# One trunk of two layers on one core: modulation sums of 1024 columns, two of them beside layer 0's modulation, paired scores, level factors from chunk tables, and eight weight pieces kept at the seam of the layers

## The chip, the core and the metric

The kernel runs on one core of a Trainium2 chip. TensorE multiplies (its weight loads are shown apart, as PEld), VectorE (DVE), ScalarE (ACT) and GpSimd (POOL) compute, SyncE (SP) issues nearly all DMAs from one queue. The metric is the device time of one execution in microseconds (us); a few runs agree within 0.3%.

## What is computed

A latent stream `x` of 256 tokens and a context of 256 tokens, 2048 features each, pass two layers. Each layer normalises, modulates, mixes, normalises again and adds to the stream:

```python
mod_l = silu_c @ w_mod[l] + b_mod[l]                 # shift, scale, gate: 3 x 2048
h_lat = rms_norm(x, g_pre[l]) * (1.0 + sc_l) + sh_l
y_lat = even_mixer(...) if l == 0 else odd_mixer(...)
x = x + gt_l * rms_norm(y_lat, g_post[l])
```

Layer 0's mixer has two branches from one projection of 9 x 1024 columns. One is differential attention with 8 heads: two softmaxes over 512 keys per head, each on 64 features, the second subtracted with a weight. The other is a gated linear recurrence (HGRN2) with 8 heads, run forwards and backwards; per head `exp(cumsum(log f))` weighs the keys and queries:

```python
att = jnp.einsum('bthk,btshk,bshk->bhts', qc, decay, kc)   # decay = exp(b_t - b_s), s <= t
s_new = jnp.exp(b_last)[..., None] * s + ...               # state over chunks of 32 tokens
```

The branches are gated and projected back to 2048 features. Layer 1 pools neighbouring tokens over 2, 4, 8 and 16 positions, with a projection before and after. All data are float32.

## The kernel before, in words

*Weight pieces.* A projection is a `Group` (L251): 512 output columns, accumulated in banks of PSUM over 8 pieces of 256 rows. `load_w` (L209) brings a piece of 512 KB by SP into one of four `w` buffers; `split` (L215) copies it to a rounded `hi` on ScalarE and subtracts on VectorE to get `lo`; `mul` (L265) makes three matmuls (L279) for each product: hi x hi, hi x lo, lo x hi. A piece has 12 matmuls of 512 columns for two token tiles, 24 for four.

*Order.* A scheduler orders each engine's instructions by priority and by the time at which it thinks them ready; `tc.high_priority(offset=...)` raises or lowers it (FILLB = -400 is low, CHAIN = 500 high). On the chip each engine keeps that fixed order. Beside the pieces of a group, `beside` (L406) steps two queues of generators: `bg`, the heads of a branch that is ready, and `fill`, modulation sums that are needed later. The numbers BD0, FD0, FH and so on (L48 to L50) are steps per piece.

*Modulation.* Layer 0's scale and shift come from `gemv` on TensorE (L305, matmuls at L318), whose 2 x 16 MB of weights are loaded in spans of 1, 1, 2, 4, 4 and 4 tiles of 128 features (`SPANS`, loop at L487). Between the loads of a span stand pieces of the three groups that start layer 0 (`starters`). The other rows, layer 1's scale and shift and both gates, come from `gemv_row` (L326): 8 loads of [256 rows x 512 columns] into two `wf` buffers, and for each row tile one instruction of VectorE that multiplies by the condition and adds to `ga` (L335, L337). A `feature_sink` (L347) then sums over partitions with small matmuls (L353), a `gate_sink` (L364) with one wide one (L374). There are 16 such rows of 512 columns; seven are queued after `hg_batch(0)` and stepped beside `da_batch(0)` and `hg_batch(1)`, five after that, four in layer 1.

*Recurrent heads* (`hg_heads`, L627, stepped beside `da_batch`). `b` is a cumulative sum that restarts every 32 tokens. The cross-half factor (level 128) and level 64 are scans of their own (`scan`, L572 to L576), `qi`, the factor of the state, two more. Levels 32 to 2 subtract on VectorE left and right halves apart (L602 to L606), exponentiate on ScalarE (L607), multiply by q (L624). Each level's 128x128 products (L648, L658) are merged into `att` on VectorE with a mask (`copy_predicated`, L663). The tag `tb` has 8 buffers.

*Attention heads* (`da_heads`, L725). For each head and token tile the scores of the two 64-feature halves (L735, three matmuls each into an `auxb` bank), maximum (L736), exponential (L740), difference (L747), transposes (L751) and the product with the values (L757), both in `auxb` too. `auxb`, `aux` have two banks each, `acc` four.

*The seam.* `close_layer` (L864) ends a layer: for the last group all pieces are first multiplied for token tile 0 and kept, then for tile 1, while tile 0 is scaled, added to the stream, squared and normalised (`normed`, L937, matmuls L944). Layer 1's first group (L967) keeps LAG = 3 pieces in the same way for tile 0 before tile 1 is there:

```python
            for k2 in range(LAG):
                kept.append((k2, g.weights(k2, where=in_y if k2 > 2 else None)))
                g.mul(*kept[-1], js=[0])
```

Of the kernel before, what the change touches and what calls it, by code (L numbers as in the profile page):

```python
# [46 lines left out]
LAG = 3  # L47
FH, FG, FO, FD0, FD1, FZ, FU = 2, .5, .5, .7, .7, .5, .5  # L48
# [6 lines left out]
def hybrid_kernel(  # L55
# [24 lines left out]
    def tinyb(n, dtype=F32):  # L80
        return alloc("tinyb", [P, n], dtype, 12)
# [111 lines left out]
    tmp = tiny(32)  # L193
# [54 lines left out]
    def in_y():  # L248
        return alloc("y", [P, 2, 512], F32R, 4), alloc("y", [P, 2, 512], F32R, 4)
# [76 lines left out]
    def gemv_row(l, col, sink):  # L326

        acc = alloc("ga", [P, 512], F32, 1)
        for k2 in range(8):
            w = load_w(w_mod[l], k2, col, "wf", 2)  # L330
            with tc.high_priority(offset=FILLB):
                for i in range(2):
                    sc = csil[:, 2 * k2 + i, 0:1]
                    if k2 + i == 0:
                        nc.vector.tensor_scalar(out=acc, in0=w[:, i, :], scalar1=sc, scalar2=None, op0=ALU.mult)  # L335
                    else:
                        nc.vector.scalar_tensor_tensor(out=acc, in0=w[:, i, :], scalar=sc, in1=acc, op0=ALU.mult,  # L337
                                                       op1=ALU.add)
            if k2 < 7:
                yield  # L340
# [23 lines left out]
    def gate_sink(l, f):  # L364
        def sink(ev):
            if f % 2 == 0:
                gtg[l, f // 2] = alloc("qT", [P, 1024], F32, 3)
            dst = gtg[l, f // 2][:, (f % 2) * 512:(f % 2) * 512 + 512]
            bb, gb = t2([P, 512]), t2([P, 512])
            cc = slice(f * 512, f * 512 + 512)  # L370
            nc.sync.dma_start(out=bb, in_=b_mod[l:l + 1, 4096 + f * 512:4608 + f * 512].to_broadcast([P, 512]))
            nc.sync.dma_start(out=gb, in_=g_post[l:l + 1, cc].to_broadcast([P, 512]))
            pt = aux([P, 512])
            nc.tensor.matmul(pt, ones[:, 0:P], ev, start=True, stop=True)  # L374
            nc.vector.tensor_tensor(out=dst, in0=pt, in1=bb, op=ALU.add)
            nc.vector.tensor_tensor(out=dst, in0=dst, in1=gb, op=ALU.mult)
        return sink
# [119 lines left out]
    work(len(pending))  # L497
# [3 lines left out]
    lvm = cst.tile([P, 8, P], U8, name="lvm")  # L501
    for i in range(0, 8, 4):
        t = t2([P, 4, P])
        nc.sync.dma_start(out=t, in_=lvlmask[:, i:i + 4, :])
        nc.vector.tensor_copy(out=lvm[:, i:i + 4, :], in_=t)
# [36 lines left out]
    def hg_logs(zc, d, gks, Ss, v_ctx):  # L542

        for h in range(4):
# [550 lines left out]
```

## Time and profile before

| | us |
|---|---|
| median of 3 runs | 1280.19 |
| lowest and highest | 1279.68, 1283.44 |
| profiled execution, its time | 1280.65 |
| profiled execution, its span | 1278.8 |
| TensorE busy | 1216.6 (95%) |
| VectorE busy | 937.1 (73%) |
| ScalarE busy | 588.1 (46%) |
| mean granted TensorE clock | 0.993 |

The span runs from the first to the last instruction; the execution's own time adds what lies around it. Busy shares are means over stages: the span has layer 0's modulation to about 228 us, layer 0's mixer to about 936 us, the seam to about 980 us and layer 1 after it. A matmul's busy time begins before the one ahead has ended, so the busy time of a row of matmuls is shorter than the sum of theirs; the granted clock is a share of full speed (1.00 is 2.4 GHz, 0.50 is 1.2).

### The profile page before, as it was taken

What the parts mean: (1) busy time and instruction counts of PE and PEld (TensorE: products, weight loads), DVE (VectorE), ACT (ScalarE), POOL (GpSimd) and SP (SyncE); (2) the same over time, 40 slices, a digit from 0 to 9 for tenths busy, and PEclk for the clock granted to TensorE, in tenths of its full rate; (3) what the DMA queues carried; (4) which work ended last, traced back from release to release, by engine and by line L of the source; (5) the groups of instructions that cost most, each with busy time, mean ns of one, the idle gap of its engine ahead of it and who ended that gap; (6) DMA issues with size and microseconds to landing.
All of it is one profiled execution on the core that took longest, in us unless ns stands there. A gap on an engine that the chain in (4) does not pass through costs nothing.

```text
span 1278.8 us, 16568 instructions
## 1 busy us (share of the span) xinstructions
PE 1216.6 (95%) x5938; PEld 958.7 (75%) x5938; DVE 937.1 (73%) x1711; ACT 588.1 (46%) x999; POOL 5.6 (0%) x59
## 2 busy tenths in 40 slices
PE   3999999999999999999999999999998999999997
PEld 2666677777788777777777777788876888888885
DVE  3554556999988656688899797888866668786654
ACT  4231324764544633234544456664456535444452
POOL 0000000000000000000000000000000000000000
PEclk9999999999999999999999999999998999999999
DMA  9988753753335447767445266767854788776553
GB/s 290 319 303 296 266 172 98 258 170 112 119 99 172 163 141 230 234 201 243 132 132 169 79 221 204 267 213 260 309 206 158 226 302 296 263 242 191 177 201 116
DMA packets 144246, 263.72 MB, mean 206 GB/s; under 512 B 8306, under 2 KB 21412, under 8 KB 144164
## 3 DMA queue, kind: packets, MB, share of 16 engines
q1 hardware_dynamic: 144164, 262.66, 61.9%
q8 instruction: 47, 0.77, 0.2%
q14 instruction: 35, 0.29, 0.1%
HBM read 260.53 MB, written 2.10 MB: 205 GB/s over the span
## 4 chain that ended last, share of the span: by engine, by line
PE 67%; DVE 16%; DMA 9%; ACT 4%; issue 3%; SPq 1%; DVEq 0%; ACTq 0%
PE acc L279 46%; PE auxb L279 8%; DMA wf<-in_w_mod_dram 5%; DVE lo L218 3%; DVE ga L337 3%; PE aux L318 3%; DVE tb L576 3%; PE auxb L658 2%; PE auxb L735 2%; ACT hi L217 2%; DMA h<-in_w_mod_dram 1%; PE auxb L757 1%; PE aux L353 1%; DMA w<-in_ev_w_out_dram 1%; DMA w<-in_ev_w_in_dram 1%
## 5 line engine op out<-in xcount | busy, mean ns | idle before, releaser
L279 PE MATMUL acc<-hi,h 128*128 128x512 f32 x1968 | 632.9, 396 | 1.0 <-ACT hi L217 1.0
L217 ACT ACTIVATE hi<-w 128x1024 fp32r<-128x1024 f32 x270 | 286.0, 1060 | 393.5 <-PE acc L279 254.8
L279 PEld LDWEIGHTS acc<-hi,h 128*128 128x128 f32 x1968 | 368.4, 188 | 84.5 <-issue 10.3
L218 DVE TENSOR_TENSOR lo<-w,hi 128x1024 fp32r<-128x1024 f32 x270 | 328.9, 1221 | 138.8 <-ACT hi L217 127.2
L279 PE MATMUL acc<-lo,h 128*128 128x512 f32 x984 | 389.1, 395 | 2.9 <-DVE lo L218 2.9
L279 PEld LDWEIGHTS acc<-lo,h 128*128 128x128 f32 x984 | 185.3, 188 | 46.2 <-issue 6.1
L337 DVE SCALAR_TENSOR_TENSOR ga<-wf,csil,ga 128x512 f32<-128x512 f32 x240 | 179.6, 748 | 46.1 <-DMA wf<-in_w_mod_dram 42.7
L279 PE MATMUL acc<-h,hi 128*128 128x512 f32 x512 | 165.9, 400 | 0.0
L279 PEld LDWEIGHTS acc<-h,hi 128*128 128x128 f32 x512 | 96.8, 191 | 19.2 <-issue 0.5
L279 PE MATMUL acc<-h,lo 128*128 128x512 f32 x256 | 102.4, 400 | 0.0
L279 PE MATMUL auxb<-h,hi 128*128 128x512 f32 x256 | 82.9, 405 | 1.1 <-DVE tb L300 1.1
L279 PEld LDWEIGHTS auxb<-h,hi 128*128 128x128 f32 x256 | 45.8, 188 | 25.2 <-issue 8.2
L300 DVE TENSOR_TENSOR tb<-auxb,tb 128x512 f32<-128x512 f32 x56 | 38.0, 688 | 30.1 <-PE auxb L279 30.0
L279 PEld LDWEIGHTS acc<-h,lo 128*128 128x128 f32 x256 | 49.0, 191 | 9.2
L279 PE MATMUL auxb<-h,lo 128*128 128x512 f32 x128 | 49.8, 394 | 0.0
L318 PE MATMUL aux<-h,tb 128*32 128x128 f32 (+2 forms) x320 | 30.1, 476 | 9.3 <-DMA h<-in_w_mod_dram 5.7
L658 PEld LDWEIGHTS auxb<-tb 128*128 128x128 f32 x224 | 29.8, 190 | 10.0 <-DVE tb L624 4.5
L658 PE MATMUL auxb<-tb 128*128 128x128 f32 x224 | 33.7, 282 | 1.2 <-DVE tb L624 0.8
L736 DVE TENSOR_REDUCE tinyb<-auxb 128x1 f32<-128x512 f32 x32 | 22.0, 687 | 15.6 <-PE auxb L735 15.5
L576 DVE TENSOR_TENSOR_SCAN tb<-ones,gk 128x63 f32<-128x63 f32 (+4 forms) x112 | 32.6, 364 | 0.0
L740 ACT ACTIVATE tb<-auxb,tinyb 128x512 f32<-128x512 f32 x32 | 21.8, 683 | 19.5 <-DVE tinyb L737 19.4
L218 DVE TENSOR_TENSOR h<-t,h 128x512 fp32r<-128x512 f32 x40 | 26.9, 685 | 2.8 <-ACT h L217 2.4
(237 smaller groups left out, 1187.7 us busy)
## 6 DMA issues: line engine op xcount, KB each, us to landing
w<-in_ev_w_in_dram SPq DMA_DIRECT2D x144, 512.0 KB, 4.0
wf<-in_w_mod_dram SPq DMA_DIRECT2D x132, 512.0 KB, 4.8
w<-in_od_w_in_dram SPq DMA_DIRECT2D x64, 512.0 KB, 4.6
h<-in_w_mod_dram SPq DMA_DIRECT2D x20, 1024.0 KB, 7.3
w<-in_ev_w_out_dram SPq DMA_DIRECT2D x32, 512.0 KB, 4.9
w<-in_od_w_out_dram SPq DMA_DIRECT2D x32, 512.0 KB, 3.4
v<-in_w_mod_dram SPq DMA_DIRECT2D x24, 256.0 KB, 3.9
h<-in_w_mod_dram SPq DMA_DIRECT2D x8, 512.0 KB, 7.0
```

The costliest lines, as they stand in the source:

```text
L217: nc.scalar.activation(out=hi, in_=src, func=AF.Copy)
L218: nc.vector.tensor_tensor(out=lo, in0=src, in1=hi.bitcast(F32), op=ALU.subtract)
L279: nc.tensor.matmul(self.ps[j], a, b, start=self.mm[j] == 1, stop=self.mm[j] == 6 * of)
L300: nc.vector.tensor_tensor(out=t, in0=ps, in1=t, op=ALU.add)
L318: nc.tensor.matmul(ps[32 * j:32 * j + 32, :], cpad[:, kt, :], w[:, i, :], start=kt < 4, stop=kt >= 12)
L337: nc.vector.scalar_tensor_tensor(out=acc, in0=w[:, i, :], scalar=sc, in1=acc, op0=ALU.mult, op1=ALU.add)
L353: nc.tensor.matmul(pt[:, b, :], ev[:, sl], sel if l == 0 else ones[:, 0:2], start=True, stop=True)
L576: nc.vector.tensor_tensor_scan(out=o, data0=ones[:, 0:n], data1=src, initial=0.0, op0=ALU.mult, op1=ALU.add)
L658: nc.tensor.matmul(pt[:, i, s, :], wk[:, sl], wq[:, sl], start=True, stop=True)
L735: nc.tensor.matmul(ps, q, k, start=n == 0, stop=n == 2)
L736: nc.vector.reduce_max(out=mx[:, m:m + 1], in_=ps, axis=AX.X)
L740: nc.scalar.activation(out=pm, in_=ps, func=AF.Exp, scale=0.125, bias=mx[:, m:m + 1], accum_out=sm[:, m:m + 1])
```

## The change

Modulation sums are 1024 columns wide: `gemv_row` loads [128 rows x 1024 columns] 16 times (512 KB each as before) and makes one VectorE instruction of each, 8 rows instead of 16. The two rows of layer 1's scale are queued before layer 0's modulation and stepped in its last two spans (1 and 2 steps after each piece) and 3 after each of the last pieces; the shift's two rows follow `hg_batch(0)`, the gates' two `hg_batch(1)`. Beside `da_batch(0)` there are no fill steps.

In `hg_heads` `kd` and `qd` are the decayed keys and queries inside chunks of 32; the factors of level 128, of level 64 and of the state are these times small tables over chunks (`chunk_tables`, `at`), level 32 is `kd` and `qd` themselves. For the other levels left and right halves are taken by one instruction through a strided view. Levels 64, 32 and 16 are copied into `att` by ScalarE block by block, without a mask. In `hg_logs` the copy of `kd` goes from VectorE to ScalarE.

In `da_heads` the six scores alternate between the halves and are kept in their order (`issue_after`); the transposes and the product with the values use `aux`. The seam keeps all 8 pieces of layer 1's first group, in buffers of seven tags, and has no fill steps there.

```diff
-FH, FG, FO, FD0, FD1, FZ, FU = 2, .5, .5, .7, .7, .5, .5
+FH, FG, FO, FD0, FD1, FZ, FU = 1.5, .5, .5, 0, .5, .5, .5
...
-    def gemv_row(l, col, sink):
-        acc = alloc("ga", [P, 512], F32, 1)
-        for k2 in range(8):
-            w = load_w(w_mod[l], k2, col, "wf", 2)
...
+    def gemv_row(l, col, sink, home=("ga", 1)):
+        acc = alloc(home[0], [P, 1024], F32, home[1])
+        for k in range(KT):
+            w = alloc("wf", [P, 1024], F32, 2)
+            nc.sync.dma_start(out=w, in_=w_mod[l][k * P:k * P + P, col:col + 1024])
+            sc = csil[:, k, 0:1]
             with tc.high_priority(offset=FILLB):
+                if k == 0:
+                    nc.vector.tensor_scalar(out=acc, in0=w, scalar1=sc, scalar2=None, op0=ALU.mult)
+                else:
+                    nc.vector.scalar_tensor_tensor(out=acc, in0=w, scalar=sc, in1=acc, op0=ALU.mult, op1=ALU.add)
+            yield
         sink(acc)
...
-    def work(n=1):
+    beside_span = {8: 1, 12: 2}
+
+    def work(n=1, steps=0):
         for _ in range(min(n, len(pending))):
             pending.pop(0)()
+            fill.step(steps)
+
+    for i in range(2):
+        fill.add(gemv_row(1, 2048 + 1024 * i, feature_sink(1, 1, 8 * i, 8), ("qT", 3)))
...
-                work()
-        work(len(pending) - LEFT)
+                work(1, beside_span.get(kt0, 0))
+        work(len(pending) - LEFT, beside_span.get(kt0, 0))
...
-    work(len(pending))
+    work(len(pending), 3)
...
+    def view(t, off, *dims):
+        return bass.AP(t.tensor, t.offset + off, [t.ap[0], *([a, n] for a, n in dims)])
+    def halves(t, h, key, o=0, n=T):
+        off, step = (o, T + h) if key else (T + o, h - T)
+        return view(t, off, (2 * h, n // (2 * h)), (step, 2), (1, h))
+    def chunk_tables(b):
+        tot = lambda c, *dims: view(b, 32 * c + 31, (T - 31, 2), *dims)
+        t = alloc("ct", [P, 48], F32, 2)
+        at = lambda k, c, *dims: view(t, 16 * k + c, *dims)
+        nc.gpsimd.memset(t, 0.0)
+        scan(at(0, 0, (1, 8)), view(b, 31, (32, 7)), 1, 7, False)
+        scan(at(0, 8, (1, 8)), view(b, T + 224, (-32, 7)), 0, 6, True)
...
+        nc.scalar.activation(out=t, in_=t, func=AF.Exp)
+        return at
...
+            n = T // (2 * h)
+            blocks = lambda t: t.rearrange("p (n two h) -> p n two h", two=2, h=h)
+            nc.vector.tensor_tensor(out=blocks(e[:, 0, :]), in0=view(b, h - 1, (2 * h, n), (T + 1, 2), (0, h)),
+                                    in1=halves(u, h, True), op=ALU.subtract)
+            nc.vector.tensor_tensor(out=blocks(e[:, 1, :]), in0=halves(b, h, False),
+                                    in1=view(b, T + h, (2 * h, n), (-T - 1, 2), (0, h)), op=ALU.subtract)
             nc.scalar.activation(out=e, in_=e, func=AF.Exp)
...
-            qi = tb([P, 2, T])
-            scan(qi[:, 0, :], gf, 0, T - 1, False)
-            scan(qi[:, 1, :], gb[:, ::-1], 0, T - 1, True)
...
+            kd, qd = tb([P, 2, T]), tb([P, 2, T])
...
+            nc.scalar.activation(out=kd, in_=kd, func=AF.Exp)
+            nc.scalar.activation(out=qd, in_=b, func=AF.Exp)
+            at = chunk_tables(b)
+            nc.vector.tensor_tensor(out=qd, in0=qd, in1=qT.unsqueeze(1).to_broadcast([P, 2, T]), op=ALU.mult)
             yield
+            att, w = tb([P, 2, 2, P]), tb([P, 2, T])
+            for k, src in enumerate((kd, qd)):
+                nc.vector.tensor_tensor(
+                    out=w[:, k, :].rearrange("p (a c k) -> p a c k", a=2, k=32),
+                    in0=view(src, k * T, ((1 - 2 * k) * T + P, 2), (32, 4), (1, 32)),
+                    in1=at(1, 8 * k, (4 + 8 - 16 * k, 2), (1, 4), (0, 32)), op=ALU.mult)
...
+                    if lv >= 16:
+                        for o in range(0, P, 2 * lv):
+                            sl = slice(o, o + 2 * lv)
+                            nc.scalar.copy(out=att[sl, 0, :, sl], in_=pt[sl, i, :, sl])
...
+                ps = [auxb([P, 512]) for _ in range(2)]
+                rows = [slice(64 * m, 64 * m + 64) for m in range(2)]
+                for n, (i, k) in enumerate(((0, 0), (0, 1), (1, 0))):
+                    for m in range(2):
+                        r = rows[m]
+                        with tc.issue_after(last.ins) if last else ExitStack():
+                            last = nc.tensor.matmul(ps[m], qT[i][r, h, sl], ks[h][k][r, :], start=n == 0, stop=n == 2)
...
-                pt = auxb([P, 4, P])
+                pt = aux([P, 4, P])
...
-                po = auxb([P, P])
+                po = aux([P, P])
...
-            for k2 in range(LAG):
-                kept.append((k2, g.weights(k2, where=in_y if k2 > 2 else None)))
+            for k2, where in enumerate((None, in_wf, in_qv, in_v, in_tb, None, None, in_h)):
+                kept.append((k2, g.weights(k2, where=where)))
                 g.mul(*kept[-1], js=[0])
             for k2, w in kept:
                 g.mul(k2, w, js=[1])
-            for k2 in range(LAG, 8):
-                g.piece(k2)
-                fill.step(1)
```

## Rows read from the trace of the kernel before

**Rows 1.** Busy time by stage: window, its length, each engine's busy us (instructions), clock, DMA.
```profile
31.00:73.00 42.00, 40.76 (x257) 25.45 (x257) 20.00 (x35) 9.04 (x14) 0.00 (x0) 1.00 0.99 334
73.00:130.00 57.00, 55.88 (x298) 36.67 (x298) 29.18 (x44) 14.68 (x21) 0.00 (x0) 1.00 0.82 288
130.00:181.00 51.00, 51.00 (x256) 33.30 (x254) 24.59 (x35) 12.66 (x18) 0.00 (x0) 1.00 0.67 227
181.00:228.00 47.00, 47.00 (x216) 38.06 (x215) 34.21 (x60) 22.94 (x39) 0.41 (x4) 1.00 0.37 117
228.00:400.00 172.00, 165.19 (x847) 134.78 (x847) 155.88 (x378) 93.61 (x192) 1.48 (x20) 1.00 0.46 147
400.00:500.00 100.00, 97.78 (x479) 75.82 (x478) 68.85 (x122) 46.63 (x96) 0.30 (x3) 1.00 0.55 178
500.00:610.00 110.00, 104.00 (x467) 84.26 (x466) 82.12 (x130) 39.45 (x66) 0.50 (x5) 0.97 0.70 230
610.00:740.00 130.00, 124.83 (x644) 101.69 (x644) 117.26 (x309) 62.20 (x137) 1.08 (x16) 1.00 0.41 129
740.00:840.00 100.00, 99.83 (x468) 75.97 (x467) 83.29 (x156) 61.65 (x109) 0.00 (x0) 1.00 0.70 229
...
936.00:980.00 44.00, 35.34 (x173) 28.46 (x172) 28.34 (x63) 26.79 (x60) 0.00 (x0) 0.92 0.41 139
```

**Rows 2.** Chain of waits, a piece of layer 1: start, length, what.
```profile
1008.22 43.55 PE acc L279 x192
```

**Rows 3.** Waits of TensorE, whole span: us in total, times, longest.
```profile
PE auxb L648 <- DVE tb L624: 8.8, 8, 2.0
...
PE aux L353 <- DVE ga L337: 4.2, 2, 2.2
```

**Rows 4.** Timeline of TensorE, six scores together: start, length, line, count.
```profile
401.42 0.97 PE L735 MATMUL auxb<-gk,qT 64*128 64x512 f32 x6
402.32 0.50 PE L279 MATMUL acc<-hi,h 128*128 128x512 f32 x1
```

**Rows 5.** Timeline of TensorE, the last place with the scores apart.
```profile
819.53 0.96 PE L735 MATMUL auxb<-gk,qT 64*128 64x512 f32 x3
820.43 0.50 PE L279 MATMUL acc<-lo,h 128*128 128x512 f32 x1
820.86 0.96 PE L735 MATMUL auxb<-gk,qT 64*128 64x512 f32 x3
821.75 0.50 PE L279 MATMUL acc<-hi,h 128*128 128x512 f32 x1
```

**Rows 6.** Groups by line and shape, VectorE: count | busy us, mean ns | idle before.
```profile
L218 DVE TENSOR_TENSOR lo<-w,hi 128x1024 fp32r<-128x1024 f32 x270 | 328.9, 1221 | 138.8 <-ACT hi L217 127.2 <-DMA w<-in_ev_w_in_dram 5.8 <-PE aux L374 3.3
L337 DVE SCALAR_TENSOR_TENSOR ga<-wf,csil,ga 128x512 f32<-128x512 f32 x240 | 179.6, 748 | 46.1 <-DMA wf<-in_w_mod_dram 42.7
...
L218 DVE TENSOR_TENSOR h<-t,h 128x512 fp32r<-128x512 f32 x40 | 26.9, 685 | 2.8 <-ACT h L217 2.4
L624 DVE TENSOR_TENSOR tb<-tb,qT 128x256 f32<-128x256 f32 x64 | 26.6, 420 | 1.6 <-ACT tb L623 1.5
...
L602 DVE TENSOR_TENSOR tb<-tb,tb 128x128 f32<-128x128 f32 x40 | 11.5, 287 | 0.0
```

**Rows 7.** The page's costliest groups: the scans of the heads, all shapes together.
```profile
L576 DVE TENSOR_TENSOR_SCAN tb<-ones,gk 128x63 f32<-128x63 f32 (+4 forms) x112 | 32.6, 364 | 0.0
```

**Rows 8.** Busy time by stage of the modulation sums alone (L337), VectorE.
```profile
228.00:400.00 172.00, 23.01 (x31) 1.00 0.46 147
```

**Rows 9.** Timeline of TensorE at the seam; in brackets the idle time before.
```profile
955.80 1.95 PE L944 MATMUL aux<-tb,gk 128*128 128x128 f32 x16
...
963.75 0.50 PE L279 MATMUL acc<-lo,h 128*128 128x512 f32 x1 [1.20 <-DVE lo L218]
...
969.73 3.78 PE L944 MATMUL aux<-tb,gk 128*128 128x128 f32 x16 [4.56 <-DVE tb L935]
```

**Rows 10.** DMA issues of the page: count, KB each, median us to landing.
```profile
wf<-in_w_mod_dram SPq DMA_DIRECT2D x132, 512.0 KB, 4.8
```

More of the change, by code (lines that the diff above doesn't have):

```diff
@@ L192, in hybrid_kernel @@
     csil = cst.tile([P, KT, 2], F32, name="csil")
-    tmp = tiny(32)
+    tmp = tb([P, 32])
     silu_el(csil, col2[:, 0:32].rearrange("p (v k) -> p k v", v=2), tmp.rearrange("p (v k) -> p k v", v=2))
@@ L246, in in_tb, with in_wf, in_qv @@
         return tuple(Two([tb([P, 512], F32R) for _ in range(2)]) for _ in range(2))
-    def in_y():
-        return alloc("y", [P, 2, 512], F32R, 4), alloc("y", [P, 2, 512], F32R, 4)
+    def in_wf():
+        return tuple(alloc("wf", [P, 2, 512], F32R, 2) for _ in range(2))
+    def in_qv():
+        return alloc("qT", [P, 2, 512], F32R, 3), Two([alloc("v", [P, 512], F32R, 6) for _ in range(2)])
     class Group:
@@ L362, in hybrid_kernel, with gate_sink @@
     gtg = {}
-    def gate_sink(l, f):
+    def gate_sink(l, f2):
         def sink(ev):
[L366 to L376, printed above, removed]
+            gtg[l, f2] = alloc("qT", [P, 1024], F32, 3)
+            for f in range(2 * f2, 2 * f2 + 2):
+                half = slice((f % 2) * 512, (f % 2) * 512 + 512)
+                dst = gtg[l, f2][:, half]
+                bb, gb = t2([P, 512]), t2([P, 512])
+                cc = slice(f * 512, f * 512 + 512)
+                nc.sync.dma_start(out=bb, in_=b_mod[l:l + 1, 4096 + f * 512:4608 + f * 512].to_broadcast([P, 512]))
+                nc.sync.dma_start(out=gb, in_=g_post[l:l + 1, cc].to_broadcast([P, 512]))
+                pt = aux([P, 512])
+                nc.tensor.matmul(pt, ones[:, 0:P], ev[:, half], start=True, stop=True)
+                nc.vector.tensor_tensor(out=dst, in0=pt, in1=bb, op=ALU.add)
+                nc.vector.tensor_tensor(out=dst, in0=dst, in1=gb, op=ALU.mult)
         return sink
@@ L496, in hybrid_kernel @@
         pending += [(lambda g=g, kt=kt, n=n: start_piece(g, kt, n)) for kt in range(kt0, kt0 + nk, n) for g in starters]
-    work(len(pending))
+    work(len(pending), 3)
     rp = cst.tile([P, 2, T], F32, name="rp")
     nc.sync.dma_start(out=rp, in_=rope)
[L501 to L505, printed above, removed]
+    lvm = cst.tile([P, 5, P], U8, name="lvm")
+    for i, n in ((3, 4), (7, 1)):
+        t = t2([P, n, P])
+        nc.sync.dma_start(out=t, in_=lvlmask[:, i:i + n, :])
+        nc.vector.tensor_copy(out=lvm[:, i - 3:i - 3 + n, :], in_=t)
     def v_tiles(g):
@@ L565, in hg_logs @@
             kd = tb([P, 2, P])
-            nc.vector.tensor_copy(out=kd, in_=pt)
+            nc.scalar.copy(out=kd, in_=pt)
             pS = auxb([P, P])
@@ L651, in hg_heads @@
             yield
+            w = tb([P, 2, T])
+            for k, src in enumerate((kd, qd)):
+                for side in range(2):
+                    row = side ^ k
+                    nc.vector.tensor_tensor(
+                        out=view(w, k * T + 64 * side, (P, 2), (32, 2), (1, 32)),
+                        in0=view(src, row * T + 64 * side, (P, 2), (32, 2), (1, 32)),
+                        in1=at(2, 8 * row + 2 * side, (4, 2), (1, 2), (0, 32)), op=ALU.mult)
+            k32 = tb([P, 4, 2, 32])
+            nc.scalar.copy(out=k32, in_=halves(kd, 32, True))
+            k32 = k32.rearrange("p n a k -> p (n a k)")
             for i0 in range(0, 8, 2):
@@ L725, in da_heads @@
     def da_heads(qT, ks, v, y, ssy):
+        last = None
         for h in range(4):
```

120 lines of the change are left out of this document (44 added, 76 removed).

## Prediction

> **What bounds the kernel now.** I read the table of busy time by stage first. From 31 us on TensorE is the engine without slack: 55.9 of 57 us, 51.0 of 51, 47.0 of 47 beside layer 0's modulation, 97.8 of 100 and 99.8 of 100 in the two stretches with the attention scores [rows 1]. The large weight matmuls cannot shrink: in the chain of waits 192 of them take 43.55 us, 0.227 us each [rows 2], and the change leaves their number alone. So time can come from two places only: matmuls that are slower than they need be, and stretches where TensorE stands. TensorE stands 172 - 165.2 = 6.8 us in 228 to 400 us and 130 - 124.8 = 5.2 us in 610 to 740 (the recurrent heads, VectorE busy 155.9 of 172 and 117.3 of 130), 6.0 us in 500 to 610 and 8.7 us in 936 to 980, the seam of the two layers, where the mean clock is also 0.92 [rows 1]. The list of waits names two of the causes: the cross-half matmul L648 waits 8.8 us in 8 places for the factors of L624, and the matmuls of the modulation's sink L353 4.2 us in 2 places for the sum on VectorE [rows 3]. The busy time of a matmul overlaps the next one's, so short stalls hide in it; I take start-to-start times where I can.
>
> **The change, part by part.** The sum is made against the profiled execution, 1280.65 us (span 1278.8), 0.46 above the median of 1280.19.
>
> *Scores (da_heads, L735).* There are 16 places, 96 matmuls over 64 rows each. In 5 of them the six already stand together with the halves alternating: from 401.42 to the next weight matmul at 402.32 is 0.90 us, so two halves run side by side [rows 4]. In the other 11 each half's three stand alone with a weight matmul between: 819.53 to 821.75 is 2.22 us, less 0.227 for that matmul is 1.99 [rows 5, 2]. The new order alternates the halves and lets nothing of the heads in between; it asks for both auxb banks at once, which the move of the transposed weights and of the output to aux leaves free. 11 x (1.99 - 0.90) = **-12.0**; ends 0, if they don't pair, and -12.0. The order is pinned, so where a first score waits, every later weight matmul in TensorE's queue waits with it; what it waits for, the scores of the place before, read by two exponentials, is done before that place's own output matmuls, after which it stands.
> The Trainium skill, TensorEngine Tiling (Array Packing), Theoretical Speedup and Key Properties, gives up to 2x for 64 rows, and a drain at each change of tiling mode. The 2x alone would be an estimate of 66 x 0.227 / 2 = 7.5 us; the rows give more, because the separate threes also pay a change of mode twice, and with that the trace agrees.
>
> *Factors of the recurrent heads.* Removed on VectorE: 14 scans a head, 32.6 us in all [rows 7]; the 128x128 subtractions, 40 + 40 + 32 + 32 + 16 + 16 = 176 at 0.287 = 50.5; 24 of 64 products with q at 0.420 = 10.1 [rows 6]. Added per head: one 128x512 (0.685, as L218's), ten 128x256 at 0.420, four 128x128 at 0.287, one more 128x512 product (0.685), six tiny ones, together about 1 (estimate from the 0.287 of 128 columns, halved): 7.7 us, 61.6 in eight heads [rows 6]. VectorE is 93.2 - 61.6 = 31.6 us lighter (two predicated copies a head not counted). POOL gets one memset of 48 columns a head where it had two (1.5 of 172 us busy). ScalarE takes over the eviction of three levels in seven small copies and one copy in the context state; it is busy 93.6 of 172 us and 62.2 of 130 [rows 1], so I cost that at nothing, and at 0.3 us a copy, 17 us, if its slack were gone. What is late next is the same matmul: the new cross-half factors still need two scans, two exponentials and two products. Of TensorE's 12.0 us I take half back, **-6**; ends -12 and +3 (a third of L648's 8.8 again, for tb buffers: b, u, kd, qd, att and w hold six of the eight).
>
> *Wide sums.* 512 columns cost 0.748; L218 grows from 0.685 to 1.221 for twice the columns, so a wide step is about 0.748 + 0.536 = 1.284 (estimate) [rows 6]. 128 of them are 164 us against 256 x 0.748 = 191: 27 us of VectorE, which is no bound and worth nothing itself. But they move: da_batch(0) has none now (before, 23.0 us of L337 in 228 to 400 us [rows 8]), and 500 to 610 us gets at most 36 steps of 512 KB where 48 stood, with half the sinks. Of the 6.0 us there I take **-3** (ends 0, -6; the sinks' 4.2 is the nearest row [rows 3]).
>
> *Two sums beside layer 0's modulation.* 34 filler steps: 6 in the span of 8 to 11 (about 73 to 130 us), 12 in the last (130 to 181), 16 after it (181 to 228); 6, 11 and 15 of them load 0.524 MB: 3.1, 5.8, 7.9 MB. The queues moved 334 GB/s at a share of 0.99 in 31 to 73 us; by that the spare room is (334 - 288) x 57 = 2.6 MB, (334 - 227) x 51 = 5.5 and (334 - 117) x 47 = 10.2 [rows 1]. 0.8 MB is short, 2.4 us. VectorE has room till 181 (24.6 of 51 busy, 14 more), and in 181 to 228 asks for 34.2 + 15 x 1.28 = 53.4 of 47 us: low priority pushes the rest into the stretch that lost its sums. TensorE's pieces there (24 matmuls, 5.4 us per 512 KB) cover some delay. I take **+3**; ends 0 (the weights wait in their four buffers) and +33 (the rival below).
> The Trainium skill, DMA: Bandwidth & Descriptors, Specifications, gives about 358 GB/s per core from HBM. By it the room would be 4.0 and 6.7 MB, nothing short, and the sum 3 us lower; the busiest of these rows is at 334, so I keep 334.
>
> *Seam.* The second half's chain (evacuate, residual, squares, norm) ends at 969.73; before it TensorE waits 1.20 and 4.56 us, and then its 16 L944 take 3.78 us, where the first half's took 1.95: the clock's cost [rows 9]. At stake: 1.2 + 4.56 + 1.83 = 7.6 us. Five more pieces held are 30 matmuls x 0.227 = 6.8 us of work that doesn't need the second half. They need 5 x 1.22 us more of VectorE before 970, where it is busy 28.3 of 44 [rows 1, 6], beside the chain; their loads now stand in SP's queue ahead of the first gate rows, which nobody needs soon. If the splits cut in, the chain slips by one or two of 1.22. I take **-5.5**; ends -7.6 and +2.4.
>
> *Sharing aux* between heads and the gated groups' transposes: **+1** (0 to +3, a wait or two like L648's, 2.0 at the longest [rows 3]). lvm, tmp, ct, tinyb: nothing on the path.
>
> Sum: -12.0 - 6 - 3 + 3 - 5.5 + 1 = -22.5; 1280.65 - 22.5 = 1258.15, by the median 1257.7: **1258**.
>
> **Rivals.**
> *SP's queue makes layer 0 late (slower).* SP serves in order, and wf has two buffers that a low-priority sum must read before the next load goes: a load lands 4.8 us after issue [rows 10], so a cadence of (4.8 + 1.28) / 2 = 3.0 us. 17 loads before 181 us are 52 us of the queue, beside 0.82 x 57 + 0.67 x 51 = 81 that it moves now, in 108 us: 25 late; the 15 after it 45 + 17 in 47, of which half counts, 8. 1280.65 - 25.5 + 33 = **1288**. It decides from 29 us late on. Against it: 18 loads don't hold the queue if the wait is over when SP gets there, and the last wf loads in that span (the late modulation rows) already share the tag.
> *Only the scores.* Factors, middle and seam give nothing, as each wait is replaced by the next in its chain: 1280.65 - 12.0 + 4 = 1272.7, by the median **1272**. For it: the head's chain keeps its length, and VectorE must split 1.22 us per piece while a half piece feeds TensorE 1.36.
> *The scores don't pair* because other matmuls get between or a bank is missing: 1258 + 12 = **1270**. Against it: the five places.
> *The stalls go entirely.* -12.0 - 12 - 6 - 7.6 + 1 = -36.6: **1244**. For it: VectorE loses 31.6 + 23 us where it is over 90% busy.
> *Gains and new waits cancel*: about **1279**.
>
> **How the numbers follow.** The forecast 0.45 (its own range 1250 to 1266), stalls gone 0.17, only the scores 0.17, no pairing 0.08, queue 0.08, cancelled 0.05. A measurement here tells 0.3%, 3.8 us, from no change: faster, below 1276.4, is 0.45 + 0.17 + 0.17 + 0.08 = 0.87, same 0.05, slower 0.08. From 1242 to 1275 leaves out the last two and the far tail of the second, under 2 in 10.
>
> **What would show it.** All 16 places with six scores in 0.90 us; L648's waits about halved and VectorE some 35 us lighter in 228 to 400 us (23.0 of sums and half of 31.6, less what is pushed in); no 2 us wait at L353; at the seam no 4.6 us wait before L944 and a clock near 1.00; in 73 to 228 us a DMA share near 0.95 and TensorE's standing time up by at most 3 to 5 us. It is wrong if layer 0's modulation ends more than 10 us later, if the threes stay apart, or if the pieces held at the seam wait for their splits.

## The result and the profile after

The changed kernel took 1295.76 us (median of 4 runs, 1292.8 to 1297.82) against 1280.1 for the kernel before: a ratio of 1.0117, interval 1.0100 to 1.0134. By that ratio it is 15 us slower; 22.5 us faster was forecast. The profiled execution took 1294.08 us, its span 1292.3.

Busy time by stage after the change (columns as in [rows 1]):

```profile
73.00:130.00 57.00, 56.30 (x299) 36.41 (x291) 33.27 (x48) 12.13 (x17) 0.00 (x0) 1.00 0.84 302
130.00:181.00 51.00, 45.68 (x219) 28.23 (x218) 30.79 (x39) 10.76 (x15) 0.00 (x0) 1.00 0.87 290
181.00:228.00 47.00, 44.93 (x199) 34.17 (x200) 36.92 (x51) 16.20 (x25) 0.12 (x1) 0.96 0.77 253
228.00:400.00 172.00, 167.88 (x848) 135.98 (x847) 147.49 (x289) 99.58 (x216) 1.24 (x11) 0.99 0.53 172
400.00:500.00 100.00, 99.42 (x483) 76.89 (x482) 50.83 (x85) 49.10 (x99) 0.10 (x1) 1.00 0.32 95
500.00:610.00 110.00, 106.93 (x489) 86.25 (x488) 63.73 (x86) 40.20 (x75) 0.69 (x7) 0.98 0.55 178
610.00:740.00 130.00, 126.68 (x653) 103.17 (x652) 100.74 (x222) 66.06 (x149) 0.28 (x2) 1.00 0.42 135
740.00:840.00 100.00, 96.10 (x466) 73.36 (x465) 68.39 (x122) 62.22 (x112) 0.00 (x0) 0.99 0.56 170
...
936.00:980.00 44.00, 37.78 (x180) 31.16 (x178) 32.68 (x66) 29.25 (x65) 0.00 (x0) 0.93 0.55 182
```

TensorE now stands 5.3 us in 130 to 181 us and 2.1 in 181 to 228, where it stood not at all before [rows 1]. VectorE has 8 us less to do in 228 to 400 us, where the prediction had some 35: 29.2 us of sums (L339) stand there, 23.0 before [rows 8]. In 400 to 500 us it has 18 less. In 740 to 840 us TensorE stands 3.9 us, before 0.2.

The chain of waits in layer 1 (start, length, what):

```profile
1153.66 11.15 PE acc L281 x48
```

48 weight matmuls in 11.15 us are 0.2323 us each; before it was 0.2268 [rows 2]. The same work, with nothing to wait for, takes 2.4% longer, and some 4320 such matmuls make 24 us of TensorE's time. It is not the clock: granted is 1.00 in both kernels from 1050 to 1250 us.

Waits of TensorE over the span (us in total, times, longest), then six scores on its timeline, then VectorE's groups by shape, then the seam:

```profile
PE aux L990 <- DVE tb L981: 6.0, 2, 5.7
PE aux L874 <- DVE y L890: 3.6, 1, 3.6
PE auxb L667 <- DVE tb L661: 3.4, 5, 1.4
PE auxb L570 <- ACT tb L567: 3.2, 3, 1.9
...
PE aux L375 <- DVE ga L339: 1.5, 1, 1.5
...
PE aux L353 <- DVE qT L339: 0.3, 1, 0.3
```

```profile
749.38 0.96 PE L782 MATMUL auxb<-gk,qT 64*128 64x512 f32 x6
750.28 0.50 PE L281 MATMUL acc<-hi,h 128*128 128x512 f32 x1
```

```profile
L217 DVE TENSOR_TENSOR lo<-w,hi 128x1024 fp32r<-128x1024 f32 x265 | 323.2, 1222 | 193.7 <-ACT hi L216 192.7
...
L339 DVE SCALAR_TENSOR_TENSOR ga<-wf,csil,ga 128x1024 f32<-128x1024 f32 x90 | 115.4, 1282 | 38.4 <-DMA wf<-in_w_mod_dram 38.1
L339 DVE SCALAR_TENSOR_TENSOR qT<-wf,csil,qT 128x1024 f32<-128x1024 f32 x30 | 38.4, 1280 | 3.5 <-DMA wf<-in_w_mod_dram 3.5
```

```profile
958.75 2.05 PE L990 MATMUL aux<-tb,gk 128*128 128x128 f32 x16 [0.29 <-DVE tb L981]
...
976.45 1.83 PE L990 MATMUL aux<-tb,gk 128*128 128x128 f32 x7 [5.67 <-DVE tb L981]
```

The cross-half matmul's wait went from 8.8 to 3.4 us and the sink's from 4.2 to 0.3 [rows 3]; the scores take 749.38 to 750.28, 0.90 us [rows 4], and 0.89 to 0.90 at all 16 places; a wide step is 1.28 us. In their place stand 3.6 us at L874, the transposes of a gated output, and 3.2 at L570. At the seam the second half still waits 5.67 us, where 4.56 stood before [rows 9].

A count through the two traces shows where the time went. The n-th weight matmul (counted from 0) starts, after less before: +0.1 us at the 192nd, +14.7 at the 576th (where the 576 matmuls of layer 0's three starting groups end), +23.4 at the 1056th, then back to +4.5 at the 2688th (862 us before), +5.3 at the 3168th, and +13.5 at the last. So there is a loss at the start, a gain in the mixer, and a second loss in layer 1. The count takes these matmuls alone; in the mixer, where the heads' matmuls stand between them, it also moves with the order.

### The profile page after: what moved, and what is told of

The parts are those of the page before. It is cut to its first block, busy times and chain, and to the rows that moved or that the text cites. A ratio compares the mean times of both kernels' runs of the same rounds, so it can differ in the third digit from the quotient of the medians.

```text
span 1292.3 us, 16256 instructions
## 1 busy us (share of the span) xinstructions
PE 1229.1 (95%) x5938; PEld 957.6 (74%) x5938; DVE 877.8 (68%) x1396; ACT 589.4 (46%) x1033; POOL 4.3 (0%) x35
## 4 chain that ended last, share of the span: by engine, by line
PE 62%; DVE 16%; DMA 11%; issue 5%; ACT 4%; SPq 1%; DVEq 0%; ACTq 0%
PE acc L281 44%; DMA wf<-in_w_mod_dram 8%; PE auxb L281 7%; DVE lo L217 4%; DVE ga L339 3%; PE aux L320 2%; ACT hi L216 1%; DMA h<-in_w_mod_dram 1%; PE auxb L693 1%; PE aux L805 1%; PE aux L353 1%; PE auxb L782 1%; PE aux L799 1%; PE aux L990 1%; DVE h L217 1%
## 5 line engine op out<-in xcount | busy, mean ns | idle before, releaser
L216 ACT ACTIVATE hi<-w 128x1024 fp32r<-128x1024 f32 x265 | 280.4, 1059 | 401.1 <-PE acc L281 273.1
L217 DVE TENSOR_TENSOR lo<-w,hi 128x1024 fp32r<-128x1024 f32 x265 | 323.2, 1222 | 193.7 <-ACT hi L216 192.7
L281 PEld LDWEIGHTS acc<-hi,h 128*128 128x128 f32 x1928 | 362.5, 190 | 89.5 <-issue 7.8
L339 DVE SCALAR_TENSOR_TENSOR ga<-wf,csil,ga 128x1024 f32<-128x1024 f32 x90 | 115.4, 1282 | 38.4 <-DMA wf<-in_w_mod_dram 38.1
L302 DVE TENSOR_TENSOR tb<-auxb,tb 128x512 f32<-128x512 f32 x56 | 38.2, 689 | 26.9 <-PE auxb L281 26.4
L339 DVE SCALAR_TENSOR_TENSOR qT<-wf,csil,qT 128x1024 f32<-128x1024 f32 x30 | 38.4, 1280 | 3.5 <-DMA wf<-in_w_mod_dram 3.5
L693 PE MATMUL auxb<-tb 128*128 128x128 f32 x192 | 29.2, 282 | 2.9 <-DVE tb L636 2.8
L281 PEld LDWEIGHTS auxb<-h,lo 128*128 128x128 f32 x128 | 24.5, 192 | 9.2 <-DVE lo L217 3.7
L324 ACT COPY t<-aux 128x512 f32<-128x512 f32 (+2 forms) x12 | 5.3, 442 | 53.1 <-PE aux L320 53.0
L216 ACT ACTIVATE h<-t 128x512 fp32r<-128x512 f32 x40 | 24.1, 623 | 11.1 <-DVE t L877 9.0
```

The costliest lines, as they stand in the source:

```text
L216: nc.scalar.activation(out=hi, in_=src, func=AF.Copy)
L217: nc.vector.tensor_tensor(out=lo, in0=src, in1=hi.bitcast(F32), op=ALU.subtract)
L281: nc.tensor.matmul(self.ps[j], a, b, start=self.mm[j] == 1, stop=self.mm[j] == 6 * of)
L302: nc.vector.tensor_tensor(out=t, in0=ps, in1=t, op=ALU.add)
L339: nc.vector.scalar_tensor_tensor(out=acc, in0=w, scalar=sc, in1=acc, op0=ALU.mult, op1=ALU.add)
L693: nc.tensor.matmul(pt[:, i, s, :], wk(s * P), wq(s * P), start=True, stop=True)
```

## The experiments

Each run's ratio is to runs of the kernel before on the same chip. A milestone (192nd, 576th, ...) is the start of that weight matmul, counted from 0, in the run's one profile.

**The step of a weight matmul.** In the kernel after, the slow step is in every stage, except where both operands lie in buffers `h` or the weights in `tb`. In the programs' layout the buffers `hi`, `lo`, `wf`, `v`, `qT` begin at the same place modulo 512 bytes as `h` before the change, and 384 bytes off after it: `tmp`'s move made the tag `tiny` smaller, and the other tables changed size. e1, e2 and e16 shift `hi` and all behind it in the kernel before by unused buffers; the order of instructions stays. e3 puts `hi` and `lo` in front of `tiny` in the kernel after, e4 moves everything there by 384 bytes and leaves the distances.

```diff
-        return alloc("tiny", [P, n], dtype, 12)
+        return alloc("tiny", [P, n], dtype, 13)      # e1; e16: 14, e2: 15
```
```diff
-    xin = []
+    xin, _ = [], [sb.tile([P, 2, 512], F32R, tag=t, bufs=3, name=f"{t}_first") for t in ("hi", "lo")]
```
```diff
-        t = alloc("ct", [P, 48], F32, 2)
+        t = cts[...]      # e4: two fixed buffers ahead of all tags
```

> The kernel before with one buffer more under the tag tiny, nothing else: same instructions in the same order, but every buffer that lies behind tiny in SBUF (wf, t2, w, hi, lo, v, S, qT, tinyb) is 128 bytes further from h. Theory (distance): the changed kernel lost about 20 us because its weights (hi, lo) no longer lie a multiple of 512 bytes from the activations (h), and every weight matmul then takes 0.232 us from start to start and not 0.227; then this kernel has the slow step too and takes about 1280 + 4300 x 0.005 = 1300 us. Rival (instructions): the slow step comes from what the changed kernel executes (its ScalarE block copies, its waits, its DMA shape); then this one stays at 1280 and at 0.227.

> The same with three buffers more under tiny: hi, lo and v are 384 bytes further, the remainder that they have in the changed kernel. Distance: a step near 0.232 and about 1300 us. Instructions: 1280 us and 0.227.

> The changed kernel with the tags hi and lo placed ahead of tiny, so that they lie a multiple of 512 bytes from h again; same instructions in the same order. Distance: the step falls from 0.232 to 0.227 us, the time from 1296 to about 1275 us, still above the forecast of 1258 by what the stages lost. Instructions: 1296 us and 0.232.

> The changed kernel with its two chunk tables moved to the front of SBUF: all large buffers stand 384 bytes higher, h exactly where it stood before the change, the distances between them as in the changed kernel. If the distance decides, 1296 us as the changed kernel; if the place of h itself decides, about 1275 us.

> The kernel before with two more unused buffers of 128 bytes, so that hi, lo and the other weight buffers stand 256 bytes off from h modulo 512 (128 and 384 bytes cost 8 and 12 us); the order of instructions is the same. If the distance counts modulo 512: a step of 0.2323 us, 1.005 to 1.010. If modulo 256: 0.2267 to 0.228 us, 1.000.

| run | distance to h | ratio | interval |
|---|---|---|---|
| e1 | 128 | 1.0058 | 1.0041 to 1.0075 |
| e16 | 256 | 0.9996 | 0.9982 to 1.0010 |
| e2 | 384 | 1.0091 | 1.0074 to 1.0107 |
| e3, after | 0 | 1.0038 | 1.0022 to 1.0053 |
| e4, after | 384 | 1.0151 | 1.0119 to 1.0183 |

Chain of waits in layer 1 of e1, e2, e16, e3 and e4:

```profile
1011.23 44.80 PE acc L279 x192
```

```profile
1011.07 44.80 PE acc L279 x192
```

```profile
1117.25 10.93 PE acc L279 x48
```

```profile
1147.66 10.90 PE acc L281 x48
```

```profile
1155.37 11.15 PE acc L281 x48
```

192 in 44.80 us are 0.2333 each (e1 and e2); 48 in 10.93 and 10.90 are 0.2277 and 0.2271; 48 in 11.15 are 0.2323. The step goes by the distance between the two operands' buffers modulo 256 bytes, not 512: 0 and 256 are fast, 128 and 384 slow; no other distance was run. Moving everything together (e4) changes nothing. Putting it right is worth 1.0117 - 1.0038 = 0.0079, 10 us. That is less than half of the 24. e1 and e2, too, had the step that was expected of them and only 7 and 12 us of the 20. e1's milestones show where the rest stays: it is 2.6 us late at the 3168th, though 3168 steps have each grown by 0.0065 us (20.6 in all), and 9.0 at the last, 6.4 more for 1152 steps (7.5). So layer 1 pays nearly in full and layer 0 little; that its waits take up the difference is a reading, no run shows it.

**The two sums beside layer 0's modulation.** In e3 the 576th milestone is still 13.2 us late. e5 is e3 with these sums behind `hg_batch(0)` and the steps per piece `FH`, `FD0`, `FD1`, as before. e17 and e18 are e3 with their loads on POOL's queue, in e18 held until 83 us.

```diff
-    for i in range(2):
-        fill.add(gemv_row(1, 2048 + 1024 * i, feature_sink(1, 1, 8 * i, 8), ("qT", 3)))
...
     hg_batch(0, g_vh, (g_zf, g_zb))
+    for i in range(2):
+        fill.add(gemv_row(1, 2048 + 1024 * i, feature_sink(1, 1, 8 * i, 8)))
```
```diff
+            if home[0] == "qT" and k < 2:      # e18 alone
+                nc.gpsimd.tensor_copy(out=w[:, 0:4], in_=sh[0][:, 4:8, 0])
-            nc.sync.dma_start(out=w, in_=...)
+            (nc.gpsimd if home[0] == "qT" else nc.sync).dma_start(out=w, in_=...)
```

> The kernel of the third run (the change with the buffers hi and lo 512-byte aligned to h, 1284.6 us), with one part undone: the two sums over layer 1's scale are not taken beside layer 0's modulation but, still over 1024 columns, behind the first HGRN batch, as before the change (FH 2, FD0 and FD1 .7). Theory (the sums beside layer 0 delay it): SP's loads and VectorE's 1.28 us steps in 73 to 235 us are gone, the last starter's matmul (576th weight matmul) comes as early as before the change, some 13 us sooner, and 9 to 14 us of that reach the end: 1271 to 1276 us. Rival A (the wide sums after 240 us cost as much wherever they stand, since their number is the same): the gain of the start is lost again between 240 and 600 us, 1282 to 1287 us. Rival B (the start's loss comes from something else of the change, such as the larger ga or the second pair of wf loads): the 576th weight matmul stays late, 1284 us.

> The kernel of the third run (aligned buffers, the two sums beside layer 0's modulation; 1.0038 of the kernel before, 576th weight matmul at 233.4 us, before 220.2) with the 32 loads of these two sums issued from POOL's queue in place of SP's. Number, size and place of the sums stay; the planner, which sees another queue, puts some operations elsewhere. Theory (the prediction's rival: a sum's load that waits for its buffer holds up the weight loads behind it in SP's queue): SP's waits for VectorE go, the 576th comes at 219 to 225 us, 0.994 to 0.999. Rival (the bytes and VectorE's 1.28 us steps cost it, whichever queue loads them): 229 to 234 us, 1.001 to 1.004.

> The kernel of the seventeenth run with POOL's queue held: POOL writes four columns of the first two wf buffers from layer 0's shift of features 4 to 7, which is ready at about 83 us, so no load of the sums goes out before. Theory (SP's in-order queue made the loss beside layer 0): the first 192 weight matmuls are on time again (105 to 108 us), the 576th comes at 219 to 225 us, and the run ends at 0.994 to 0.999 of the kernel before. Rival (the sums' bytes and VectorE's steps cost it on any queue): the 576th at 229 to 234 us, 1.001 to 1.005.

e5: 0.9963 (0.9939 to 0.9986), the 576th at 219.3 us, before 220.2. The sums there cost 1.0038 - 0.9963 = 0.0075, 9.6 us, more than behind `hg_batch(0)`. This version beats both kernels. e17: 1.0042 (1.0028 to 1.0056); POOL's timeline shows its loads leaving from 21.6 us on, 12 of them by 71 us, where the DMA share was 0.99 already [rows 1], and the 192nd came 15.5 us late:

```profile
21.60 1.62 POOL L333 DMA_DIRECT2D wf<-in_w_mod_dram  x2 [19.15 <-ACT wf L425]
30.26 0.53 POOL L333 DMA_DIRECT2D wf<-in_w_mod_dram  x1 [7.04 <-DVE qT L337]
...
70.99 0.53 POOL L333 DMA_DIRECT2D wf<-in_w_mod_dram  x1 [4.55 <-DVE qT L339]
170.50 1.12 POOL L333 DMA_DIRECT2D wf<-in_w_mod_dram  x2 [98.98 <-PE aux L320]
```

From the 192nd to the 576th it then lost 2.4 us, where e3 lost 14.0. That seemed to speak for SP's queue, but from 71 to 170 us no sum was loaded at all. e18 decides. It gave 1.0074 (1.0058 to 1.0089), the 192nd at 111.2 us, 4.6 late, and the 576th at 236.8, past the rival's range: the theory falls. Stages of e5, then e18:

```profile
73.00:130.00 57.00, 56.54 (x301) 37.30 (x294) 30.05 (x45) 15.20 (x20) 0.00 (x0) 1.00 0.84 293
130.00:181.00 51.00, 51.00 (x258) 33.45 (x257) 24.38 (x37) 12.18 (x17) 0.00 (x0) 1.00 0.67 225
181.00:228.00 47.00, 47.00 (x212) 37.83 (x211) 34.34 (x57) 23.19 (x40) 0.57 (x4) 1.00 0.40 115
```

```profile
73.00:130.00 57.00, 53.57 (x259) 34.61 (x252) 34.18 (x46) 12.50 (x17) 6.28 (x13) 0.97 0.90 325
130.00:181.00 51.00, 46.26 (x212) 28.05 (x212) 30.34 (x41) 12.08 (x16) 2.65 (x5) 0.97 0.79 278
181.00:228.00 47.00, 46.48 (x231) 36.49 (x230) 34.85 (x46) 14.49 (x20) 6.49 (x13) 1.00 0.66 221
```

What was late changed its name. In e3 SP stands 22.8 us at buffers that a sum has yet to read, and ScalarE waits 57.0 us for weights, where it waits 29.3 in e5. In e18 ScalarE's wait is 38.0; instead VectorE, whose order is fixed, stands 24.3 us at the sums for their loads (4.6 in e3), and the starters' sums on VectorE (L302) behind them hold up TensorE's weight loads for 12.9 us (7.9 in e3). POOL's loads land 5.6 us after issue in the median, SP's in e3 5.3, so the other queue is not slower by itself. Waits of 73 to 235 us (in total, times, longest), two of e3, one of e5, one of e18:

```profile
ACT hi L216 <- DMA w<-in_ev_w_in_dram: 57.0, 10, 10.0
```

```profile
SPq L333 <- DVE qT L339: 22.8, 14, 3.6
```

```profile
ACT hi L216 <- DMA w<-in_ev_w_in_dram: 29.3, 6, 7.1
```

```profile
DVE qT L341 <- DMA wf<-in_w_mod_dram: 24.3, 13, 3.4
```

So SP's queue alone is not the cause; the sums cost their time in this stretch by either queue. Whether bytes or VectorE's steps weigh more stays open.

**The seam.** e6 and e7 are e3 and e5 with the old seam, e9 is e7 without the steps of the sums behind its pieces, e13 is e9 with one of the three held pieces in `wf`, e14 is e5 with 7 held pieces and none in `wf`.

```diff
-            for k2, where in enumerate((None, in_wf, in_qv, in_v, in_tb, None, None, in_h)):
+            for k2 in range(3):                                 # e6, e7, e9
+            for k2, where in enumerate((None, in_wf, None)):    # e13
...
+            for k2 in range(3, 8):
+                g.piece(k2)
+                fill.step(1)                                    # e6, e7; not in e9, e13
```

> The kernel of the third run (1284.6 us), with the seam between the layers as before the change (3 pieces held, then whole pieces with a step of the gate's sums behind each). Theory (the 8 held pieces gave nothing, since their splits stand between the steps of the chain that makes the second half's input): 1283 to 1286 us, with the wait before the second half of normed at 4.6 us again and 3 to 5 us of waits behind it. Rival (they give the 5.5 us that the prediction put on them, and something else took these back): 1288 to 1291 us. A third case (they cost more than they give): 1279 to 1282 us.

> Both of the last two at once: aligned buffers, pinned scores, table-made factors and wide sums, without the sums beside layer 0 and with the old seam. If the two parts add up: the time of the run without the early sums plus the difference that the old seam made. With theory and theory 1270 to 1276 us, under the kernel before (1280.2); with rival A 1282 to 1287 us.

> The kernel of the fifth run (aligned buffers, sums behind the first HGRN batch; 0.9963 of the kernel before) with the old seam of 3 held pieces, but without the step of the gate's sums behind each of the five pieces that follow. Theory (what the old seam loses are these steps: VectorE stood 5.4 us at one of them for its wf load, between two operations of the chain that makes the input): the chain keeps its order, 0.996 to 0.998. Rival (the 8 held pieces cover the waits): as with the old seam, 1.000 to 1.003.

> The kernel of the ninth run (3 held pieces, 1.0051 of the kernel before) with the second of the three held pieces in the two wf buffers. No sum of the gates can load until that piece is done with, so no step of theirs stands in VectorE's order in the first half's chain. Theory (the seam's loss is these steps, waiting there 6.1 us for wf; how many pieces are held matters little): 0.996 to 0.999. Rival (eight held pieces cover the chain's waits): 1.003 to 1.006.

> The kernel of the fifth run (8 held pieces, 0.9963) with 7 held pieces, the one that was in wf left out and done after the second half's input is there. The sums' loads can start in the seam again. Theory (steps of the sums stand in the chain again): 1.000 to 1.004. Rival (the pieces cover the waits): 0.996 to 0.998.

| run | held | one in wf | ratio | interval |
|---|---|---|---|---|
| e6 | 3 | no | 1.0084 | 1.0057 to 1.0110 |
| e7 | 3 | no | 1.0013 | 0.9992 to 1.0034 |
| e9 | 3 | no | 1.0051 | 1.0033 to 1.0070 |
| e14 | 7 | no | 1.0028 | 1.0013 to 1.0042 |
| e13 | 3 | yes | 0.9970 | 0.9951 to 0.9989 |
| e5 | 8 | yes | 0.9963 | 0.9939 to 0.9986 |

Undoing the early sums and undoing the seam add up: e5 with the difference of e6 and e3 makes 0.9963 + 0.0046 = 1.0009, where e7, with both undone, has 1.0013. My reading of e3, that the new seam gave nothing, fell with e6 and e7; so did the next, that program order keeps the sums out, with e9. VectorE's timeline at the first half's chain (L923 to L186), e9 and then e13; in brackets the idle time before:

```profile
935.68 0.15 DVE L923 TENSOR_REDUCE tiny<-ssq 128x1 f32<-128x4 f32 x1
935.86 0.15 DVE L185 TENSOR_SCALAR tiny<-tiny 128x1 f32<-128x1 f32 x1
942.11 1.28 DVE L339 SCALAR_TENSOR_TENSOR ga<-wf,csil,ga 128x1024 f32<-128x1024 f32 x1 [6.10 <-DMA wf<-in_w_mod_dram]
943.32 0.15 DVE L186 SCALAR_TENSOR_TENSOR tiny<-tiny 128x1 f32<-128x1 f32 x1
```

```profile
937.55 0.15 DVE L923 TENSOR_REDUCE tiny<-ssq 128x1 f32<-128x4 f32 x1
937.73 0.15 DVE L185 TENSOR_SCALAR tiny<-tiny 128x1 f32<-128x1 f32 x1
938.29 0.16 DVE L186 SCALAR_TENSOR_TENSOR tiny<-tiny 128x1 f32<-128x1 f32 x1 [0.41 <-ACT tiny L184]
```

In e9 a sum of layer 1's gates stands between two tiny operations of the chain and waits 6.10 us there for its load; in e13, 0.41 us lie in its place. The scheduler can put it there as long as a `wf` buffer is free for its load (e9, e14); a held piece in `wf` keeps the sums away (e13, e5); the five other pieces add nothing that shows (0.9963 against 0.9970). In e14 a sum stands in the chain with a wait of 2.36 us, and in e5's chain none stands.

**The other parts, one at a time.** e8 is the kernel before with the new scores alone, e15 the same with the seam of e13. e10, e11 and e12 are e5 with, in turn, the sums over 512 columns, the heads' factors and the scores as before the change.

```diff
+                        with tc.issue_after(last.ins) if last else ExitStack():
+                            last = nc.tensor.matmul(ps[m], qT[i][r, h, sl], ks[h][k][r, :], start=n == 0, stop=n == 2)
```

> The kernel before with one part of the change alone: the differential attention's six score matmuls in the written order, two halves of the array in turn, and the transposes and the product with v out of the other pool of banks. Buffers stay where they were, so a weight matmul's step stays at 0.227 us. Theory (the prediction's term of 12 us holds, and the change's other parts lose it): six scores take 0.9 us at all 16 places, 1267 to 1271 us. Rival (the scores gain time on TensorE, but where they stand beside layer work that waits for VectorE or for loads, half of it is lost): 1272 to 1276 us. Third case (order was no limit): 1280 us.

> The kernel of the eighth run (the kernel before with the pinned scores alone, 1.0021) with one of the 3 held pieces of the seam in wf and no step of the sums behind the pieces that follow. In that run the 2688th weight matmul came 3.4 us earlier and the seam then took 10 us back. Theory (the sums' steps in the chain took it): 0.994 to 0.998, the scores' gain and perhaps a few us of the seam's own. Rival (the seam waits for something else, such as its loads): 1.000 to 1.003.

> The kernel of the fifth run (0.9963 of the kernel before) with the sums over 512 columns again, as before the change, eight pairs of steps for each row; nothing else. Prediction's term (the wide sums take some 60 us off VectorE and give 3 us): 0.998 to 1.000. Rival A (VectorE isn't the limit where the sums stand, so their width gives nothing): 0.995 to 0.998. Rival B (steps of 1.28 us in VectorE's order hold others up longer, as the 1.85 and 1.79 us at the transposes of the gated outputs at 816 and 839 us): narrow is better, 0.991 to 0.995.

> The kernel of the fifth run (0.9963 of the kernel before) with the HGRN heads' factors as before the change (scans, subtractions and exponentials by level). Prediction's term (6 us, with the waits before the cross-half matmuls): 1.000 to 1.002. Rival (the waits return, but matmuls of other work fill them or the planner hides them): 0.996 to 0.998. Other side (the tables cost more than the scans): under 0.995.

> The kernel of the fifth run (0.9963 of the kernel before) with the scores in the planner's order again. By TensorE's own rows the pinned order took the 96 scores from 24.2 us to 14.3 us. If all of that reaches the end: 1.004. If half: 1.000. If none, as the run of the scores alone suggests (1.0021 with the old seam): 0.996. Theory: half to all, since the seam that swallowed the gain there is the new one here.

e8: 1.0021 (1.0001 to 1.0040), slower if anything, which none of the three cases had; e15: 0.9980 (0.9961 to 1.0000). e8's 2688th milestone is 3.4 us early and its 3168th 6.5 late; in e15 these are 3.4 and 0.6 early. VectorE in e8's seam:

```profile
948.88 2.74 DVE L885 SCALAR_TENSOR_TENSOR gk<-y,tiny,gk 128x512 f32<-128x512 f32 x4
954.07 1.54 DVE L337 SCALAR_TENSOR_TENSOR ga<-wf,csil,ga 128x512 f32<-128x512 f32 x2 [2.45 <-DMA wf<-in_w_mod_dram]
955.52 0.15 DVE L937 TENSOR_REDUCE tiny<-ss 128x1 f32<-128x4 f32 x1
955.64 0.75 DVE L337 SCALAR_TENSOR_TENSOR ga<-wf,csil,ga 128x512 f32<-128x512 f32 x1
```

In the kernel before no sum stands in this chain; a change in the attention heads alone was enough for the scheduler to put sums (L337) between L885 and the chain's next reduction. e10 came to 0.9984 (0.9964 to 1.0004), e11 to 0.9980 (0.9967 to 0.9992), e12 to 0.9991 (0.9975 to 1.0008). So in e5's setting the scores gave 0.9991 - 0.9963 = 0.0028 (3.6 us), the wide sums 0.0021 (2.7), the factors 0.0017 (2.2), each uncertain by 3 to 4 us.

The wide sums also lose in layer 1. From the 3168th to the last weight matmul the four runs with 512-column sums and the fast step (e8, e10, e15, e16) take at most 0.6 us more than the kernel before, the eleven with wide sums and `hi` and `lo` aligned 1.6 to 7.6 more. e5 is 11.2 us ahead of the kernel before at the 3168th and 6.1 at the last; e10, which differs from it in the width alone, is 5.0 and 4.7 ahead. TensorE's wait in e5, 990 to 1275 us, for which e10 has no like:

```profile
PE acc L281 <- DVE lo L217: 3.2, 5, 1.1
```

The splits of weights come late there; that a step of 1.28 us in front of them is the reason was not tested.

Where did the gains in the mixer go? The chain of waits by line, 400 to 960 us, of the kernel before and of e5:

```profile
by line: PE acc L279 39.9%; DMA wf<-in_w_mod_dram 10.4%; DVE ga L337 5.6%; issue 5.0%; DVE lo L218 4.5%; PE auxb L735 4.0%; DVE tb L576 3.3%; ACT hi L217 2.4%; PE auxb L757 2.3%; PE auxb L658 2.2%; DMA w<-in_ev_w_out_dram 2.0%; PE auxb L751
```

```profile
by line: PE acc L281 32.2%; DMA wf<-in_w_mod_dram 18.2%; DVE ga L339 7.8%; issue 5.7%; DVE lo L217 3.6%; PE aux L802 2.1%; DMA w<-in_ev_w_out_dram 1.8%; PE auxb L779 1.8%; PE aux L796 1.4%; DVE h L217 1.3%; PE aux L353 1.2%; ACT hi L216 1.1
```

The modulation sums, a load of `wf` and the step on it, make 10.4 + 5.6 = 16% of that chain before and 18.2 + 7.8 = 26% in e5: what the other parts give up there is taken over by sums that wait for their loads. That is read from the chain; no run took the sums away.

## Why the prediction was wrong

*"The large weight matmuls cannot shrink ... the change leaves their number alone."* This step failed first. I kept 0.227 us for all of them, and moved buffers were costed at "nothing on the path" (lvm, tmp, ct, tinyb). The matmuls' step grew to 0.2323, worth 10 us at the end (e3), a term that the sum did not have. It is not the largest part of the miss: from 22.5 us faster to 15 slower is 37.5, of which 10 are the step, 9.6 - 3 = 6.6 the two sums, and 25.5 - 4.7 = 20.8 gains of the other terms that did not reach the end.

*Two sums beside layer 0, +3.* That they make layer 0 late was in the rivals, the size not in the sum: 14.7 us at the 576th milestone (13.2 in e3), past the 10 us that were to show the prediction wrong, and 9.6 at the end. I compared bytes and busy time by stage with what was free in it, and found room; but a low-priority sum in a fixed order holds up what stands behind it. Nor were the 334 GB/s of that sum the most that the queues move, nor the 358 set beside it: e17 moved 360 and 382 in 31 to 52 and 52 to 73 us. The rival's reason, SP's queue, did not hold either as the only one (e18), and its 33 us were far too many.

*Scores, -12.0.* Right on TensorE: from a place's first score to the next matmul the 96 scores' steps went from 24.2 to 14.3 us, and 11 lone entries at about 0.2 us [rows 5] go too, 12.1 in all. At the end it was 3.6 +- 3.6 us. I counted time on TensorE as time at the end.

*Factors, -6, and wide sums, -3.* L648's waits more than halved and L353's went, as said, and VectorE's busy time fell from 937.1 to 877.8 us, 59.3, where the terms had 31.6 + 27. The end got 2.2 and 2.7, neither told from nothing. The sums' term counts 500 to 610 us and leaves out layer 1, where their width loses some of what it gives.

*Seam, -5.5.* Against the kernel before, nothing: the wait is 5.67 us where 4.56 was, the clock 0.93, not near 1.00. A split did cut in, as the prediction feared: VectorE in the kernel after, second half of the chain:

```profile
973.54 0.15 DVE L185 TENSOR_SCALAR tiny<-tiny 128x1 f32<-128x1 f32 x1
974.30 1.23 DVE L217 TENSOR_TENSOR h<-w,h 128x1024 fp32r<-128x1024 f32 x1 [0.60 <-ACT h L216]
975.44 0.15 DVE L186 SCALAR_TENSOR_TENSOR tiny<-tiny 128x1 f32<-128x1 f32 x1
```

The split of the piece in `h` stands between L185 and L186 and takes 1.14 us of the chain (974.30 to 975.44). The seam's other effect, a hold on `wf`, I did not see; it saved 6 to 11 us (e6, e7, e9) that the other parts would have cost there.

*Sharing aux, +1.* L874 waits 3.6 us, once, for VectorE's y, not for a bank.

With aligned buffers and the sums later (e5) the rest of the change is 0.0037 (4.7 us) faster than the kernel before, where the prediction's terms for it come to 25.5. The terms found one at a time have intervals too wide to be added up.

## What to carry to other kernels

Before you trust a duration from the trace of before, ask whether the change moves its operands: a change in the size of small tables shifted every large buffer, and TensorE's stream got 2.4% slower. Filler work is not free because an engine has room in the mean: in a fixed order it stands in front of something, so find what stands behind it, and hold its buffers where a chain must not be cut. A gain in one stage is a gain at the end only if the chain of waits there does not run through the filler.

## What the runs showed of the hardware

A matmul of 128x128 by 128x512 started every 0.227 us when the buffers of its two operands lay 0 or 256 bytes apart in a partition, modulo 512, and every 0.232 to 0.233 us when 128 or 384 (e1, e2, e16). In e3 single pieces in `v`, `wf` and `qT`, 384 bytes off, took 0.2315 to 0.2332 at the seam, beside 0.2271 for `hi`; those in `tb`, at distance 0, took 0.2293, which the distance does not explain. The Trainium skill, SBUF — State Buffer, A bandwidth-pool intuition that's wrong, gives weight loads a read port of their own; by that alone the distance would not matter, and these runs show that it does. Why it does, no run shows.
